# Padding the tiles that TensorE reads, so that pools begin at multiples of 128 bytes and some tiles step through the residues modulo 512

## The chip, the cores and the metric

The kernel runs on one core of a Trainium2 chip. The metric is device time in microseconds (us) of one execution. Times of single instructions are given in nanoseconds (ns). Where this text speaks of an address, it means the byte offset of a buffer within a partition of the on-chip memory (SBUF); all 128 partitions have the same layout.

## The reference, cut to what matters

One sequence of 512 tokens with 1024 channels goes through two blocks. All values are float32.

```python
# first block, layer kind 0: modulation by c, short gated convolution, squared-relu MLP
a = modulate(rmsnorm(h, g_pre), mod[0], mod[1])
h = h + mod[2] * rmsnorm(short_gated_conv(a, sc_w_in, sc_conv, sc_w_out), g_post)
f = squared_relu_mlp(modulate(rmsnorm(h, g_pre_ff), mod[3], mod[4]), mlp_w_in, mlp_w_out)
h = h + mod[5] * rmsnorm(f, g_post_ff)
# second block
x = x + even_mixer(rms_norm(x, g), ...)      # 8 heads of attention with forget gates, pooling
x = x + conv_ffn(rms_norm(x, g), ...)        # up 1024 -> 2 * 2816, 3-tap convolution, down
x = x + conformer_conv(rms_norm(x, g), ...)  # 31-tap depthwise convolution, layer norm
x = x + conv_ffn(rms_norm(x, g), ...)
```

## The kernel before, in words

**Layout.** Channels lie on the partitions and tokens along the free axis, so an activation is a list of tiles of 128 channels x 512 tokens (2048 bytes in each partition).

**Products in parts.** Every float32 product is made of three products in the type float32r. An activation is split into a high and a low part (`part_pair`, then `cut_value` or `cut_scaled`), a weight block likewise (`Stream.cut`, L86). `prod3` (L458) then issues three matmuls of 512 columns: high weight x high activation (L461), high weight x low activation (L462), low weight x high activation (L463). The weight is the stationary operand, a 128 x 128 block (512 bytes in each partition), which TensorE loads while the matmul before it runs; the activation is the moving operand, streamed in 512 columns. `in_block`, `out_block` and `late1_half` call `prod3` over the channel blocks; `lead_blocks` (L486, L487, L489), `tok_prod` (L1125 to L1127, where the weight moves and the activation stands still) and `taps` (L1632 to L1634, the depthwise convolution as products with diagonal matrices) issue the same kind of matmul by themselves.

**Names.** The tiles of the pool `xa` are the inputs of the layers: `a0h` to `a7l` in the first block, `e0h` to `e7l` before the attention, `n0h` to `n7l` before the feed-forwards and the convolution module, and `mp` for the pooled part. `h` are the hidden tiles of the first block's MLP (pool `hp`), `f` those of the two feed-forwards (pools `hp0` and `hp1`, function `ffn`, L1495), `u` those of the first output projection (pool `ua`), `s` those after the layer norm (pool `slp`). `whi` and `wlo` are the split weights (pool `wsp`, six buffers each), `ma` the attention's results, `cuh` and `cul` the inputs of the depthwise convolution with `dh` and `dl` as their diagonal weights (pool `cp`), `pth` and `ptl` the turned probabilities (pool `at`).

**Order.** The order is written out by hand. SP issues the weight loads, ScalarE and VectorE split them ahead of their use, TensorE works through the blocks. Eight PSUM banks are used in turn.

**Addresses.** Pools lie one behind the other in the order in which they are opened, from byte 1152 on; a pool that is closed gives its space to the next. Each buffer is rounded up to 32 bytes. Adding up the sizes gives where the operands of TensorE begin, modulo 512:

| operand | before, modulo 512 |
|---|---|
| `xa` tiles (`a`, `e`, `n`, `mp`), `whi`, `wlo` | 384, all of them |
| `u`, `h`, `f`, `s` | 160, all of them |
| `ma` | 448 (six), 192 (two) |
| `pth`, `ptl`, the value tiles | 480 |
| `dh`, `dl` | 96 |
| `cuh` / `cul` (a tap adds 4 bytes) | 480 and 96 / 224 and 352 |
| `identr` | 416 |

The blocks within a weight tile are 512 bytes apart, so they all have the residue of their tile.

Of the kernel before, what the change touches and what calls it, by code (L numbers as in the profile page):

```python
# [15 lines left out]
P = 128  # L16
D = 1024
T = 512
# [18 lines left out]
# columns of the packed per-channel parameters  # L37
# [14 lines left out]
# order of the first projection's blocks: c, v, b of each channel block  # L52
# [7 lines left out]
def ksplit(k0, k1):  # L60
    """pieces of at most eight k blocks"""
    n = -(-(k1 - k0) // 8)
    step = -(-(k1 - k0) // n)
    return [(k, min(k + step, k1)) for k in range(k0, k1, step)]


class Stream:
    """Weights in the order in which they are used: loaded, then split into two float32r parts."""
# [17 lines left out]
    def cut(self, n, late=False):  # L86
        """the second parts may be left for later"""
        nc = self.nc
        while self.n_cut < min(n, len(self.chunks)):
            self.load(self.n_cut + 1)  # L90
            t, w = self.staged.pop(self.n_cut)
            hi = self.pool.tile([P, 1024], F32R, tag="whi", name="whi", bufs=self.n_split)
            lo = self.pool.tile([P, 1024], F32R, tag="wlo", name="wlo", bufs=self.n_split)
            nc.scalar.copy(hi[:, :w], t[:, :w])  # L94
            self.late.append((lo[:, :w], t[:, :w], hi[:, :w].bitcast(F32)))
            self.parts[self.n_cut] = (hi, lo)
            self.n_cut += 1
        if not late:
            self.finish()
# [13 lines left out]
    def ahead(self, lag=1, late=False):  # L113
        """to be called when the products of all the chunks taken, but the last lag, have been issued"""
        self.cut(self.used + self.n_split - lag, late)
# [3 lines left out]
def fused(ctx: ExitStack, tc: tile.TileContext, a, out: bass.AP):  # L119
# [19 lines left out]
    # ---- the order in which weights are used  # L139
# [45 lines left out]
    # ---- constants and parameters  # L185
# [20 lines left out]
    par = const.tile([P, NPAR], F32, name="par")  # L206
# [25 lines left out]
    still = xa.tile([P, T], F32R, tag="xa", name="still")  # L232
# [3 lines left out]
    # ---- helpers  # L236
    def run(steps, others=()):
        """a chain of steps, with other work put between them"""
        others = list(others)
        while True:  # L240
            try:
                next(steps)
            except StopIteration as e:
                res = e.value
                break
            if others:
                others.pop(0)()
        for f in others:
            f()
        return res  # L250

    def rsqrt_steps(src, n, scale, name, late=None, eps=True, out=None):
        """1 / sqrt(src * scale + EPS): a seed from the exponent, a step of the third order, one of Newton's"""
        v = src
        if eps:
            v = small.tile([P, 64], F32, tag="rv", name="rv")[:, :n]
            V.tensor_scalar(v, src, scale, EPS, op0=ALU.mult, op1=ALU.add)
            yield
        y = small.tile([P, 64], F32, tag=f"ry{name}", name="ry")[:, :n]
        V.tensor_scalar(y.bitcast(I32), v.bitcast(I32), 1, None, op0=ALU.logical_shift_right)  # L260
        hv = small.tile([P, 64], F32, tag="rh", name="rh")[:, :n]
        V.tensor_scalar(hv, v, -9.0 / 128.0, None, op0=ALU.mult)
        yield
        V.tensor_scalar(y.bitcast(I32), y.bitcast(I32), -1.0, float(0x5F3759DF), op0=ALU.mult, op1=ALU.add)
        yield
        t = small.tile([P, 64], F32, tag="rt", name="rt")[:, :n]
        V.tensor_mul(t, y, y)
        yield
        V.tensor_mul(t, t, v)
        yield  # L270
        V.scalar_tensor_tensor(t, t, -10.0 / 3.0, t, op0=ALU.add, op1=ALU.mult)
        yield
        V.scalar_tensor_tensor(y, t, 5.0, y, op0=ALU.add, op1=ALU.mult)
        yield
        V.tensor_mul(t, y, y)
        V.tensor_scalar(y, y, 0.375, None, op0=ALU.mult)
        yield
        V.tensor_mul(t, t, hv)
        if late:
            late()  # L280
        yield
        out = y if out is None else out
        V.scalar_tensor_tensor(out, t, 1.5, y, op0=ALU.add, op1=ALU.mult)
        return out
# [4 lines left out]
    class Sums:  # L289
        """sums over the channels, by token: over the blocks first, then over the partitions"""  # L290
# [44 lines left out]
    class Total:  # L335
        """[token, tile] for a sum; the last block's terms may be added over the partitions"""
# [12 lines left out]
        def copy(self):  # L349
            self.t = small.tile([P, NT], F32, tag="tot", name="tot", bufs=6)  # L350
# [15 lines left out]
    class HalfTotals:  # L366
        """the same for several sums and a half of the tokens; t is all of them, [token, sum, tile]"""
# [41 lines left out]
    def second_norm_steps(r, sxy, syy, sxx):  # L409
        """of x + r * G y, r being y's norm: from the sums of x G y, (G y)^2 and the mean of x^2 with EPS"""  # L410
# [12 lines left out]
    def turned(r):  # L423
        """[token, tile] to [any partition, token]"""
# [13 lines left out]
    def warm(n, src):  # L438
        """n products of no use, while TensorE would wait: an idle one's clock is halved"""
# [4 lines left out]
    def part_pair(name, pool=None, tag="xa"):  # L444
        pool = pool or xa
        return (pool.tile([P, T], F32R, tag=tag, name=name + "h"), pool.tile([P, T], F32R, tag=tag, name=name + "l"))

    def cut_value(dst, src):
        """two float32r parts of src"""
# [3 lines left out]
    def cut_scaled(dst, src, g, p=P):  # L453
        """two float32r parts of src * g, g by partition"""
# [3 lines left out]
    def prod3(ps, w, o, act, first, last):  # L458
        """ps += w[:, o:o+128].T @ act, without the product of the two low parts"""
# [5 lines left out]
    def in_block(acts, between=None):  # L465
        """a block of 128 outputs over all the channel blocks"""
# [7 lines left out]
    def lead_blocks(acts_of, n):  # L474
        """n such blocks at once, channel block by channel block, as those are made"""
# [16 lines left out]
    def out_halves(acts, k0, k1):  # L492
        """the same by halves of the tokens, one after the other"""
# [18 lines left out]
    # ================= first block: modulation and the short gated convolution  # L512
    mod = const.tile([P, 48], F32, name="mod")
# [8 lines left out]
    # the modulation: a column of it on each partition, the sum over its rows along the free axis;  # L522
    # on VectorE, and up to a limit on GpSimd and ScalarE
# [11 lines left out]
    def limit(b, m):  # L535
        """of the shift all is left to GpSimd, at first a half, and of the first scale a half"""
# [31 lines left out]
    def modulated(t, sc, sh, b):  # L568
        """scaled, shifted, and the first of its two parts"""
# [6 lines left out]
    def modulated_first(t, sc, sh, b):  # L576
        """the same, the first part as early as may be"""
# [76 lines left out]
    # the rest of the modulation, in pieces between the blocks  # L654
# [66 lines left out]
    # ---- output projection, post norm, residual  # L721
# [14 lines left out]
    def sums1(b, s, ps):  # L736
        """what remains is left for VectorE"""
# [26 lines left out]
    # the last blocks, by halves of the tokens: the first half's norms are made during the second's products  # L764
# [104 lines left out]
    def second_half():  # L869
        """True before steps on TensorE"""  # L870
# [56 lines left out]
    # ================= squared relu MLP  # L927
# [45 lines left out]
    # the last blocks, by halves of the tokens: the first half's norm is made during the second's products  # L973
# [75 lines left out]
    # the first of the pooled blocks' products, by halves too  # L1049
# [10 lines left out]
    def second_half():  # L1060
        """the second half's norm, between the first half's products"""
# [55 lines left out]
    # ================= second block, layer 0: forgetting attention and pooling  # L1117
# [14 lines left out]
    # pooling  # L1132
# [18 lines left out]
    # queries and keys, raw, with the sums of squares of their heads  # L1151
    qk, ssqk = [], at.tile([P, 2 * NT * NH], F32, name="ssqk")
    rr = at.tile([P, NT], F32, name="rr")
# [16 lines left out]
    def head_norms(i):  # L1170
        """norms of the heads: of the raw sums, the token's own norm squared goes with them"""
# [38 lines left out]
    # forget gates: by head, turned to tokens  # L1210
# [26 lines left out]
    # sums of the gates over tokens  # L1237
# [14 lines left out]
    # attention, head by head  # L1252
# [23 lines left out]
    # values  # L1276
    touch = at.tile([P, 1], F32, name="touch")
# [23 lines left out]
    # values, by token  # L1301
# [11 lines left out]
    # where a tile of queries lies in three banks  # L1313
# [83 lines left out]
    # the pooled part of the output goes to the residual while heads are on their way  # L1397
# [20 lines left out]
    def residual_next(b, ps, gain):  # L1418
        """the residual with a new part, and what the next layer takes of it; its end is left for later"""
# [18 lines left out]
    # the attention's part of the output; the last two heads' products come last  # L1438
# [30 lines left out]
    # ================= gated feed-forward with a causal convolution of three taps  # L1469
    def ffn(l, next_gain):  # L1470
# [9 lines left out]
        def pair(n, pg, pv, rb):  # L1480
# [14 lines left out]
            hid[n] = part_pair(f"f{n}", hp, "hp")  # L1495
# [48 lines left out]
    # ================= layer 1: convolution module  # L1544
# [7 lines left out]
    whi = cp.tile([P, CW * KB], F32R, name="dwh", bufs=1)  # L1552
    wlo = cp.tile([P, CW * KB], F32R, name="dwl", bufs=1)
# [16 lines left out]
    # on GpSimd some taps, multiplied by ScalarE, and the bias  # L1570
# [50 lines left out]
    def taps(i, k0=0, k1=CW, between=None):  # L1621
        """some of the taps on TensorE"""
# [16 lines left out]
    def dwconv(i, k0=0, k1=CW):  # L1639
        ps, n = ps_dw[i], n_pe[i] + n_pool[i]  # L1640

        # the other taps, in two sums
# [20 lines left out]
    # the norm's sums, of the channels less their first block's mean  # L1663
# [98 lines left out]
def _blocks(w):  # L1762
    """[K, N] to [N / 128, 128 rows of a k block, K / 128 * 128]"""
# [4 lines left out]
def _columns(v):  # L1768
    """[..., n * 128] to [128, ... * n]"""
    return v.reshape(-1, P).T  # L1770
# [81 lines left out]
```

## Time and profile before

| | |
|---|---|
| median of 3 runs | 1734.66 us (1733.01 to 1735.14) |
| span of the profiled execution (first to last instruction) | 1729.1 us |
| TensorE busy with matmuls | 1699.6 us, 98% of the span, 7919 matmuls |
| VectorE, ScalarE, GpSimd busy | 1100.1, 763.3, 207.2 us |
| mean granted TensorE clock | 0.997 of full speed |

Of the profiled execution the span alone is shown; the median of the runs is 5.6 us longer than it, which is taken as what lies around the span. A matmul's duration in the profile is longer than the distance from its start to the next one's, since matmuls are pipelined and their ends are modelled: what a matmul costs is read from start to start.

### The profile page before, as it was taken

What the parts mean: (1) busy time and instruction counts of PE and PEld (TensorE: products, weight loads), DVE (VectorE), ACT (ScalarE), POOL (GpSimd) and SP (SyncE); (2) the same over time, 40 slices, a digit from 0 to 9 for tenths busy, and PEclk for the clock granted to TensorE, in tenths of its full rate; (3) what the DMA queues carried; (4) which work ended last, traced back from release to release, by engine and by line L of the source; (5) the groups of instructions that cost most, each with busy time, mean ns of one, the idle gap of its engine ahead of it and who ended that gap; (6) DMA issues with size and microseconds to landing.
All of it is one profiled execution on the core that took longest, in us unless ns stands there. A gap on an engine that the chain in (4) does not pass through costs nothing.

```text
span 1729.1 us, 20739 instructions
## 1 busy us (share of the span) xinstructions
PE 1699.6 (98%) x7919; PEld 1404.0 (81%) x7919; DVE 1100.1 (64%) x1717; ACT 763.3 (44%) x1256; POOL 207.2 (12%) x184
## 2 busy tenths in 40 slices
PE   8999899999999999999999999999999999999999
PEld 6788788888888887888888888888887888888887
DVE  6877887245244776855875377557987587636752
ACT  4533454234233335763543244347885344323430
POOL 3100630000003500000000000006880000000000
PEclk9999999999999999999999999999999999999999
DMA  7476405332323132201323322332120223232232
GB/s 290 146 262 213 139 21 177 114 104 67 123 75 96 62 105 85 74 25 49 107 93 93 122 73 90 97 119 86 50 73 1 97 86 98 91 116 95 92 97 71
DMA packets 53669, 176.13 MB, mean 102 GB/s; under 512 B 6081, under 2 KB 6337, under 8 KB 52546
## 3 DMA queue, kind: packets, MB, share of 16 engines
q1 hardware_dynamic: 53570, 174.82, 30.4%
q8 instruction: 62, 1.02, 0.2%
q14 instruction: 37, 0.30, 0.1%
HBM read 172.69 MB, written 2.10 MB: 101 GB/s over the span
## 4 chain that ended last, share of the span: by engine, by line
PE 90%; DVE 6%; ACT 1%; issue 1%; POOL 0%; DMA 0%; POOLq 0%; ACTq 0%; DVEq 0%
PE ps L461 25%; PE ps L463 25%; PE ps L462 25%; PE ps L1125 1%; PE ps L1127 1%; PE ps L1126 1%; PE ps L486 1%; PE ps L487 1%; PE ps L489 1%; PE ps_dw L1632 1%; PE ps_dw L1633 1%; PE ps_dw L1634 1%; DVE ada L533 1%; DVE wlo L103 1%; PE ps_ss L343 1%
## 5 line engine op out<-in xcount | busy, mean ns | idle before, releaser
L103 DVE TENSOR_TENSOR wlo<-stage,whi 128x1024 fp32r<-128x1024 f32 (+3 forms) x311 | 339.9, 1119 | 80.9 <-ACT whi L94 79.8
L94 ACT CAST whi<-stage 128x1024 fp32r<-128x1024 f32 (+3 forms) x313 | 288.6, 947 | 176.1 <-DMA stage<-in_down 49.8
L1486 ACT ACTIVATE zo<-z,par 128x512 f32<-128x512 f32 x88 | 70.3, 814 | 157.3 <-DVE z L1484 157.3
L1490 DVE SCALAR_TENSOR_TENSOR zo<-z,par,zo 128x510 f32<-128x510 f32 (+1 forms) x176 | 123.4, 746 | 10.8 <-ACT zo L1486 10.8
L1484 DVE TENSOR_TENSOR z<-ps,rbc 128x512 f32<-128x512 f32 x88 | 59.2, 686 | 72.4 <-PE ps L463 68.9
L306 POOL TENSOR_TENSOR acc<-acc,term 128x512 f32<-128x512 f32 (+1 forms) x34 | 45.6, 1352 | 458.1 <-ACT term L310 449.3
L1579 POOL TENSOR_TENSOR po<-po,pr 128x512 f32<-128x512 f32 x55 | 73.1, 1330 | 18.2 <-ACT pr L1578 14.5
L1493 ACT ACTIVATE zo<-zo 128x512 f32<-128x512 f32 x44 | 27.9, 633 | 66.2 <-DVE zo L1490 66.2
L533 DVE SCALAR_TENSOR_TENSOR ada<-ada,cs 128x1024 f32<-128x1024 f32 (+1 forms) x42 | 52.6, 1259 | 6.2 <-DMA ada<-in_ada 6.2
L1531 DVE TENSOR_TENSOR x<-x,ps 128x512 f32<-128x512 f32 x16 | 11.0, 688 | 71.2 <-PE ps L463 71.2
L935 DVE TENSOR_TENSOR r<-r 128x512 f32<-128x512 f32 x32 | 22.1, 690 | 47.1 <-ACT r L933 47.1
L1587 POOL MEMSET cu<- 128x30 f32 x8 | 1.0, 125 | 390.1 <-PE ps L463 390.1
L933 ACT ACTIVATE r<-ps 128x512 f32<-128x512 f32 x32 | 19.1, 595 | 61.3 <-PE ps L463 57.1
L966 DVE TENSOR_TENSOR y<-y,ps 128x512 f32<-128x512 f32 x14 | 9.6, 687 | 55.2 <-PE ps L463 55.2
L1420 DVE TENSOR_TENSOR x<-x,ps 128x512 f32<-128x512 f32 x24 | 16.4, 683 | 38.3 <-PE ps L463 38.3
L461 PE MATMUL ps<-n7h,whi 128*128 128x512 f32 x104 | 40.7, 391 | 0.0
L463 PE MATMUL ps<-n7h,wlo 128*128 128x512 f32 x104 | 40.5, 390 | 0.0
L462 PE MATMUL ps<-n7l,whi 128*128 128x512 f32 x104 | 40.5, 389 | 0.0
L1578 ACT ACTIVATE pr<-cu,par 128x512 f32<-128x512 f32 x55 | 38.9, 711 | 2.8 <-POOL po L1579 2.8
L461 PE MATMUL ps<-n0h,whi 128*128 128x512 f32 x96 | 38.2, 398 | 0.0
L463 PE MATMUL ps<-n0h,wlo 128*128 128x512 f32 x96 | 37.4, 390 | 0.0
L463 PE MATMUL ps<-n1h,wlo 128*128 128x512 f32 x96 | 37.4, 390 | 0.0
(1382 smaller groups left out, 5092.0 us busy)
## 6 DMA issues: line engine op xcount, KB each, us to landing
stage<-in_up SPq DMA_DIRECT2D x88, 512.0 KB, 3.8
ada<-in_ada SPq DMA_DIRECT2D x32, 512.0 KB, 4.6
stage<-in_mlp_in SPq DMA_DIRECT2D x32, 512.0 KB, 3.6
stage<-in_down SPq DMA_DIRECT2D x32, 384.0 KB, 3.1
stage<-in_pw SPq DMA_DIRECT2D x24, 512.0 KB, 3.7
stage<-in_down SPq DMA_DIRECT2D x32, 320.0 KB, 3.3
stage<-in_mlp_out SPq DMA_DIRECT2D x28, 320.0 KB, 3.2
stage<-in_sc_in SPq DMA_DIRECT2D x17, 512.0 KB, 3.7
```

Source lines behind the costliest of these rows:

```text
L94: nc.scalar.copy(hi[:, :w], t[:, :w])
L103: (engine or self.nc.vector).tensor_sub(lo, t, hi)
L306: self.engine.tensor_add(self.acc[:, s], self.acc[:, s], t)
L461: PE.matmul(ps, hi, act[0], start=first, stop=False)
L462: PE.matmul(ps, hi, act[1], start=False, stop=False)
L463: PE.matmul(ps, lo, act[0], start=False, stop=last)
L533: V.scalar_tensor_tensor(t[:, s], t[:, s], 1.0, cs[:, s], op0=ALU.mult, op1=ALU.mult, accum_out=to)
L1484: V.tensor_mul(z, ps, rb)
L1486: S.activation(o, z, AF.Identity, bias=col(fcb, j), scale=col(fcw, 2 * 2 * FB + j))
L1490: V.scalar_tensor_tensor(o[:, s:], z[:, :T - s], col(fcw, (2 - s) * 2 * FB + j), o[:, s:], op0=ALU.mult, op1=ALU.add)
L1578: S.activation(pr, u, AF.Copy, scale=w)
L1579: G.tensor_add(po[i], po[i], pr)
```

## The change

Nothing is computed otherwise, and no instruction is added, removed or moved. Tiles become longer:

- `par`, `mod`, `rr`, `touch` (of the pool `at`), `dwh`, `dwl` and the tag `tot` (nine buffers for six) are lengthened, so that the pools behind them begin at multiples of 128 bytes.
- `whi` and `wlo` get 64 bytes more each, tiles of `xa` 32 bytes more, the `f` tiles (now under the tag `fp`) 32 bytes more; the `f` tiles with an odd number begin 16 bytes into their buffer.

```diff
+LINE = 32
...
-            hi = self.pool.tile([P, 1024], F32R, tag="whi", name="whi", bufs=self.n_split)
-            lo = self.pool.tile([P, 1024], F32R, tag="wlo", name="wlo", bufs=self.n_split)
+            hi = self.pool.tile([P, 1024 + 16], F32R, tag="whi", name="whi", bufs=self.n_split)
+            lo = self.pool.tile([P, 1024 + 16], F32R, tag="wlo", name="wlo", bufs=self.n_split)
...
-    par = const.tile([P, NPAR], F32, name="par")
+    par = const.tile([P, -(-NPAR // LINE) * LINE], F32, name="par")[:, :NPAR]
...
-    still = xa.tile([P, T], F32R, tag="xa", name="still")
+    still = xa.tile([P, T + 8], F32R, tag="xa", name="still")[:, :T]
...
-            self.t = small.tile([P, NT], F32, tag="tot", name="tot", bufs=6)
+            self.t = small.tile([P, NT], F32, tag="tot", name="tot", bufs=9)
...
-        pool = pool or xa
+        if pool is None or tag == "fp":
+            wide = (pool or xa).tile
+            o = 4 * (int(name[1:]) % 2) if tag == "fp" else 0
+            return tuple(wide([P, T + 8], F32R, tag=tag, name=name + p)[:, o:o + T] for p in "hl")
         return (pool.tile([P, T], F32R, tag=tag, name=name + "h"), pool.tile([P, T], F32R, tag=tag, name=name + "l"))
...
-    mod = const.tile([P, 48], F32, name="mod")
+    mod = const.tile([P, 56], F32, name="mod")[:, :48]
...
-    rr = at.tile([P, NT], F32, name="rr")
+    rr = at.tile([P, LINE], F32, name="rr")[:, :NT]
...
-    touch = at.tile([P, 1], F32, name="touch")
+    touch = at.tile([P, LINE], F32, name="touch")[:, :1]
...
-            hid[n] = part_pair(f"f{n}", hp, "hp")
+            hid[n] = part_pair(f"f{n}", hp, "fp")
...
-    whi = cp.tile([P, CW * KB], F32R, name="dwh", bufs=1)
-    wlo = cp.tile([P, CW * KB], F32R, name="dwl", bufs=1)
+    whi = cp.tile([P, 8 * LINE], F32R, name="dwh", bufs=1)[:, :CW * KB]
+    wlo = cp.tile([P, 8 * LINE], F32R, name="dwl", bufs=1)[:, :CW * KB]
```

The removed comments and docstrings are left out here. Adding up the new sizes in the same way gives:

| operand | after, modulo 512 |
|---|---|
| `xa` tiles, the sixteen buffers | 0, 32, 64, ... 480, one each |
| `whi`, the six buffers | 0, 64, 128, 192, 256, 320 |
| `wlo`, the six buffers | 384, 448, 0, 64, 128, 192 |
| `u`, `h`, `s` | 128, all of them |
| `f`, the 24 buffers | 128, 160, 192, ... in steps of 32; 16 more for an odd number |
| `ma` | 0 (six), 256 (two) |
| `pth`, `ptl`, the value tiles | 128 |
| `dh`, `dl` | 128 |
| `cuh` / `cul` (a tap adds 4 bytes) | 0 and 128 / 256 and 384 |
| `identr` | 0 |

## Rows read from the trace of the kernel before

**Rows 1.** The page, part 1: busy us, share of the span, instructions.
```profile
PE 1699.6 (98%) x7919; PEld 1404.0 (81%) x7919; DVE 1100.1 (64%) x1717; ACT 763.3 (44%) x1256; POOL 207.2 (12%) x184
```

**Rows 2.** The page, part 4: shares of the chain that ended last.
```profile
PE 90%; DVE 6%; ACT 1%; issue 1%; POOL 0%; DMA 0%; POOLq 0%; ACTq 0%; DVEq 0%
```

**Rows 3.** Groups by line, PE: shapes, count, then busy us and mean ns.
```profile
L461 PE MATMUL ps<-n7h,whi 128*128 128x512 f32 x104 | 40.7, 391 | 0.0
L463 PE MATMUL ps<-n7h,wlo 128*128 128x512 f32 x104 | 40.5, 390 | 0.0
...
L462 PE MATMUL ps<-n3l,whi 128*128 128x512 f32 x96 | 37.3, 389 | 0.0
...
L461 PE MATMUL ps<-a1h,whi 128*128 128x512 f32 x44 | 17.1, 390 | 0.0
...
L1127 PE MATMUL ps<-whi,e5l 128*128 128x512 f32 x12 | 4.7, 390 | 0.0
```

**Rows 4.** The same view, the `f` tiles: first and last kind.
```profile
L461 PE MATMUL ps<-f1h,whi 128*128 128x512 f32 x16 | 6.3, 395 | 0.0
...
L463 PE MATMUL ps<-f21h,wlo 128*128 128x512 f32 x15 | 5.9, 395 | 0.0
```

**Rows 5.** One tile's instructions, `h5h`, `s1h`: count, duration min/median/max ns.
```profile
L461 PE MATMUL ps<-h5h,whi x8: 393/395/397, 296.5 to 350.4; 128*128 128x512 f32 x8
...
L461 PE MATMUL ps<-s1h,whi x4: 396/396/396, 1339.9 to 1356.7; 128*128 128x512 f32 x4
```

**Rows 6.** Timeline of PE (start us, us), from 999.76 us on.
```profile
999.76 0.39 PE L461 MATMUL ps<-n5h,whi 128*128 128x512 f32 x1
999.99 0.39 PE L462 MATMUL ps<-n5l,whi 128*128 128x512 f32 x1
...
1008.83 0.39 PE L462 MATMUL ps<-n2l,whi 128*128 128x512 f32 x1
```

**Rows 7.** Timeline of PE, from 923.84 us on.
```profile
923.84 0.40 PE L461 MATMUL ps<-f0h,whi 128*128 128x512 f32 x1
...
932.48 0.40 PE L462 MATMUL ps<-f1l,whi 128*128 128x512 f32 x1
```

**Rows 8.** Timeline of PE in the attention's output, from 781.55 us on.
```profile
781.55 0.39 PE L461 MATMUL ps<-ma,whi 128*128 128x512 f32 x1
...
788.88 0.39 PE L463 MATMUL ps<-ma,wlo 128*128 128x512 f32 x1
```

**Rows 9.** Timeline of PE in the depthwise taps, from 1231.82 us on.
```profile
1231.82 0.39 PE L1632 MATMUL ps_dw<-cuh,dh 128*128 128x512 f32 x1
...
1235.77 0.40 PE L1634 MATMUL ps_dw<-cuh,dl 128*128 128x512 f32 x1
```

**Rows 10.** Two tiles' instructions: the least and the greatest durations.
```profile
L462 PE MATMUL ps<-n0l,whi x96: 387/389/398, 815.2 to 1658.9; 128*128 128x512 f32 x96
...
L1633 PE MATMUL ps_dw<-cul,dh x83: 389/396/404, 1179.3 to 1306.8; 128*128 128x512 f32 x83
```

**Rows 11.** Timeline of PE, matmuls of 256 columns, `u` and `a` tiles.
```profile
192.97 0.28 PE L461 MATMUL ps<-u0h,whi 128*128 128x256 f32 x1
...
193.91 0.28 PE L463 MATMUL ps<-u2h,wlo 128*128 128x256 f32 x1
...
240.14 0.28 PE L915 MATMUL ps<-a7h,whi 128*128 128x256 f32 x1
...
240.98 0.28 PE L915 MATMUL ps<-a0h,whi 128*128 128x256 f32 x1
```

**Rows 12.** Stretches: length, then busy us (instructions) of PE, granted clock, DMA.
```profile
924.00:980.00 56.00, 56.00 (x242) 1.00 0.33 102
1000.00:1080.00 80.00, 80.00 (x354) 1.00 0.27 88
```

## Prediction

> **What bounds the kernel now.** I read the busy times first. TensorE is busy with matmuls for 98% of the span, and the next engine, VectorE, for 64% [rows 1]. The chain that ended last says the same from its end: 90% of it is TensorE, and no line of it is a transfer [rows 2]. So TensorE's stream of matmuls is the kernel, and a change that adds, removes and moves no instruction can act on the time in one way alone: by the distance from the start of one matmul to the start of the next. The granted clock is 1.00 in the stretches that I compare, so this is the 2.4 GHz level throughout [rows 12]; 512 columns at 2.4 GHz are 213.3 ns, one column in a cycle.
>
> The next view is the grouping by line with shapes kept apart. The same three lines issue the same 128 x 512 matmul all over the kernel, and yet two levels show: 389 to 391 ns where the moving tile is `n`, `a` or a weight against `e` [rows 3], 395 ns where it is `f` [rows 4], and 395 to 396 ns where it is `h` or `s` [rows 5]. The ends are modelled, so I take the starts from the timeline. From 999.76 to 1008.83 us there are 40 steps of `n` matmuls: 9.07 / 40 = 226.75 ns [rows 6]. From 923.84 to 932.48 us there are 37 steps of `f`: 8.64 / 37 = 233.5 ns [rows 7]. A duration in these rows is thus some 162 ns more than the step, in both groups. The attention's output has 32 steps of `ma` in 7.33 us, 229.1 ns [rows 8], and the depthwise taps 17 steps in 3.95 us, 232.4 ns [rows 9].
>
> What differs between these groups is not the weight's address, which is 384 modulo 512 for `n`, `f` and `ma` alike, but the moving tile's: 384 for `n` and `a` (a multiple of 128, and the weight's own residue), 448 and 192 for `ma` (odd multiples of 64), 160 for `f`, `h`, `s` and `u` (an odd multiple of 32), and anything in steps of 4 bytes for the taps. By rows, then: multiples of 128 cost 226.75 ns, odd multiples of 64 cost 229.1, odd multiples of 32 cost 233.5, a mixture 232.4.
>
> **The change part by part.** The pads of `par`, `mod`, `tot`, `rr`, `touch`, `dwh` and `dwl` cost nothing themselves: no instruction reads the added bytes, and VectorE, ScalarE and the transfers handle as many elements as before. The three more buffers of `tot` could only remove waits, and on the chain that ended last TensorE waits for almost nothing. What they do is to move what lies behind them. Four groups of matmuls come out of this.
>
> *Group 1, what reads `xa`.* Counting the rows of the grouped view, 2519 matmuls of 512 columns read `n`, 1224 `a`, 96 `mp` and 48 `e` as moving operand, and 288 have `e` as the standing one: 4175. Today both operands are at 384. Afterwards the sixteen buffers step by 32, so that half of the tiles stand at multiples of 64 and half at odd multiples of 32, and the weights at multiples of 64. For the first half I take the middle of the two rows, (226.75 + 229.1) / 2 = 227.9 ns, for the second half 233.5 ns [rows 6 to 8]; the mean is 230.7 ns. That is 3.95 ns more in each of 4175: +16.5 us.
>
> *Group 2, `h`, `s` and `u`.* 708 + 192 + 120 = 1020 matmuls of 512 columns move from 160 to 128, with weights at multiples of 64: from 233.5 to 227.9 ns, -5.6 ns each, -5.7 us.
>
> *Group 3, `f`.* 1023 matmuls. Of an even-numbered pair one tile is at a multiple of 64 and the other at an odd multiple of 32, 230.7 ns as in group 1; the odd-numbered pairs begin 16 bytes off, and the nearest row is that of the taps, 232.4 ns [rows 9]. The mean, 231.5 ns, is 2.0 ns less than today: -2.0 us.
>
> *Group 4, the rest.* In the taps, weights and moving tiles shift by the same 32 bytes, so they keep their distance; I leave them at nothing, and 249 of them at 1 ns would be 0.25 us. Some 710 matmuls have 256 columns: those of `u` now take 0.94 us for 8 steps, 117.5 ns, those of `a` 0.84 us for 7, 120 ns [rows 11]. These levels stand the other way round than at 512 columns; a change of 2.5 ns in all of them would be 1.8 us either way, and I take nothing.
>
> The sum is 16.5 - 5.7 - 2.0 = +8.8 us. The profiled execution's span of 1729.1 us becomes 1737.9, and with the 5.6 us that the median has beyond that span, 1743.5 us.
>
> The bounds. No row shows varied addresses in the order that the change makes, where the distance between weight and moving tile is another one in nearly every matmul. The dearest nearby view is that nothing settles and all matmuls of groups 1 to 3 cost what `f` costs now: 6.75 x 4175 = +28.2 us, 1763 us. With the taps' 232.4 ns in group 1 and the rest as above it is +23.6 - 7.7 = +15.9 us, 1750.6 us. The cheapest is the least duration on record, 387 ns against a usual 389 [rows 10], a step of some 224.7 ns: with that everywhere, 2.05 x 4175 + 8.8 x 2043 = 8.6 + 18.0 = 26.6 us less, 1708 us. I take the middle values because they are the rows of steady stretches; the greatest durations of the taps, 404 ns [rows 10], are single ones.
>
> **The rivals.** *The equal residues are the trouble, and spreading them is the cure (faster).* A step of 226.75 ns is 13.4 ns more than the columns need, although nothing is waited for. If that excess arises where the weight's read meets the moving tile's read at the same residue, then `xa` pays it in every matmul today and will pay less afterwards. For it speaks that at 256 columns the unequal pair (160 and 384) takes 117.5 ns and the equal one 120 [rows 11]. Against it: at 512 columns every unequal pair on record is dearer than the equal one [rows 6 to 9]. It decides the sign when group 1 comes to less than 226.75 + 7.7 / 4.175 = 228.6 ns; with the least step on record throughout, it gives 1708 us. The Trainium skill (page "TensorE: Matmul & The Clock Gate", section "Wait — 56ns, not 53.3ns?") gives about 215.7 ns for back-to-back matmuls of 512 columns at the full clock; no step of 512 columns in this trace is as short, and by that figure the sum would be near 1652 us, an estimate.
>
> *Only the alignment counts, and the spread is harmless (faster, smaller).* Then `xa` stays at 226.75 ns, group 2 gains up to 6.75 ns, 6.9 us, and group 3 between 2.0 and 6.9 us: 1721 to 1726 us, 1723 in the middle. It wants a tile at an odd multiple of 32 to cost no more than one at 384, which `f`, `h` and `s` deny with their weights at 384; with the weights of other residues it is not shown.
>
> *Addresses have no effect (the same).* The two levels would then come from what else runs beside the matmuls. Against it, `n` and `f` alternate within the same feed-forward, at a similar share of the transfers, 0.27 and 0.33 [rows 12], and `h` and `s`, in other stages with other neighbours, have the level of `f` [rows 5]. It gives 1734.7 us. The Trainium skill (same page, section "Step-by-step: what each phase is for") says that TensorE reads its standing and its moving operand through two independent ports, so that loading the next weights takes no read bandwidth from the running matmul. By that rule no residue could matter and the sum would be zero; the trace does not agree, with 226.75 against 233.5 ns for the same instruction.
>
> **How the numbers follow.** The slower case has 0.48: the rows carry it, but its largest term rests on pairs of addresses that no row shows. The first rival has 0.19, the second 0.23, the third 0.10. So faster by over 0.2% (3.5 us, about what a measurement of this kernel tells from no change) is 0.42, within it 0.10, slower 0.48. The predicted time is that of the likeliest case, 1743.5 us; its own range is 1738 to 1757 us. The range that should hold 8 in 10 has to take in both signs: from 1708, the cheapest case, to 1757 us, short of the dearest bound.
>
> **What would show it.** If I am right, the rows of `n` and `a` in the grouped view rise from 389 to some 393 ns and differ from tile to tile, those of `h`, `s` and `u` fall to 390 to 391, those of `f` to 393, and the steps in the timeline follow. VectorE's, ScalarE's and the transfers' times do not change. I am wrong if the `n` rows stay at 389 (second rival) or fall below it (first), or if `h` stays at 395, which would mean that the multiple of 128 was not what made `n` cheap.

## The result, and the profile after

The changed kernel takes 1747.76 us (median of 4 runs, 1745.41 to 1749.85) against 1733.84 us of the kernel before (4 runs, 1730.77 to 1735.14): a ratio of 1.0091, 95% interval 1.0079 to 1.0103, slower by 0.9%. The prediction was 1743.5 us and slower. The medians differ by 13.9 us, and the interval stands for 13.7 to 17.9 us. The span of the profiled execution grew by 16.9 us, from 1729.1 to 1746.0 us; the mean granted clock of these two executions was 0.997 and 0.992.

The page of the changed kernel, parts 1 and 4, which answer to [rows 1, 2]:

```profile
PE 1715.8 (98%) x7919; PEld 1406.6 (81%) x7919; DVE 1102.0 (63%) x1717; ACT 763.0 (44%) x1256; POOL 208.7 (12%) x184
...
PE 91%; DVE 6%; ACT 1%; issue 1%; POOL 0%; DMA 0%; POOLq 0%; ACTq 0%; DVEq 0%
```

The same number of instructions on every engine, and TensorE alone is longer: by 16.2 us, nearly all of the span's 16.9. The weight loads are not (1404.0 before, 1406.6 now). So the place to look is the step from one matmul to the next, as before. The groups by line, which answer to [rows 3, 4]; the edit moves the lines by five, so that `prod3` is now at L466 to L468:

```profile
L466 PE MATMUL ps<-n7h,whi 128*128 128x512 f32 x104 | 41.0, 394 | 0.0
...
L467 PE MATMUL ps<-n3l,whi 128*128 128x512 f32 x96 | 37.8, 394 | 0.0
...
L466 PE MATMUL ps<-a1h,whi 128*128 128x512 f32 x44 | 17.4, 396 | 0.0
...
L468 PE MATMUL ps<-f21h,wlo 128*128 128x512 f32 x15 | 5.9, 396 | 0.0
...
L1132 PE MATMUL ps<-whi,e5l 128*128 128x512 f32 x12 | 4.7, 395 | 0.0
```

The 389 to 391 ns of `n`, `a` and `e` have become 394 to 396; `f` stands where it stood. Two tiles' instructions (least, median and greatest duration), which answer to [rows 5]:

```profile
L466 PE MATMUL ps<-h5h,whi x8: 392/394/398, 296.3 to 349.8; 128*128 128x512 f32 x8
...
L466 PE MATMUL ps<-s1h,whi x4: 392/398/404, 1352.3 to 1369.1; 128*128 128x512 f32 x4
```

`h` and `s`, now at a multiple of 128, have not come down to 390: the medians were 395 and 396 and are 394 and 398, only with more spread. The timeline gives the steps. For `n` (compare [rows 6]) two rounds of 24 matmuls, for `f` [rows 7] 61 steps, for `h` five rounds of 33:

```profile
1007.97 0.39 PE L466 MATMUL ps<-n0h,whi 128*128 128x512 f32 x1
...
1019.08 0.40 PE L466 MATMUL ps<-n0h,whi 128*128 128x512 f32 x1
```

```profile
930.81 0.40 PE L466 MATMUL ps<-f1h,whi 128*128 128x512 f32 x1
...
944.93 0.40 PE L467 MATMUL ps<-f10l,whi 128*128 128x512 f32 x1
```

```profile
296.27 0.39 PE L466 MATMUL ps<-h5h,whi 128*128 128x512 f32 x1
...
334.53 0.40 PE L466 MATMUL ps<-h5h,whi 128*128 128x512 f32 x1
```

`n`: 11.11 / 48 = 231.5 ns, where it was 226.75. `f`: 14.12 / 61 = 231.5 ns, where it was 233.5. `h`: 38.26 / 165 = 231.9 ns; the same five rounds took 38.50 us before, 233.3 ns. The granted clock is 1.00 in these stretches, the 2.4 GHz level, so the columns still take 213.3 ns. Three groups with three different layouts have ended at one level, some 231.5 to 232 ns. With the counts of the prediction that is 4.75 x 4175 = +19.8 us for group 1, -1.4 x 1020 = -1.4 us for group 2 and -2.0 x 1023 = -2.0 us for group 3: +16.4 us, and the span has grown by 16.9. The stretches are typical: over all steps under 300 ns in the two traces `n` goes from 226.9 to 231.8 ns in the mean, `a` from 227.0 to 232.0, `h` from 233.4 to 231.5 and `f` from 233.4 to 231.8.

### The profile page after: what moved, and what is told of

Read it like the earlier page. It is cut to its first block, busy times and chain, and to the rows that moved or that the text cites. A ratio compares the mean times of both kernels' runs of the same rounds, so it can differ in the third digit from the quotient of the medians.

```text
span 1746.0 us, 20739 instructions
## 1 busy us (share of the span) xinstructions
PE 1715.8 (98%) x7919; PEld 1406.6 (81%) x7919; DVE 1102.0 (63%) x1717; ACT 763.0 (44%) x1256; POOL 208.7 (12%) x184
## 4 chain that ended last, share of the span: by engine, by line
PE 91%; DVE 6%; ACT 1%; issue 1%; POOL 0%; DMA 0%; POOLq 0%; ACTq 0%; DVEq 0%
PE ps L466 25%; PE ps L467 25%; PE ps L468 25%; PE ps L1130 1%; PE ps L1131 1%; PE ps L1132 1%; PE ps L491 1%; PE ps L492 1%; PE ps L494 1%; PE ps_dw L1637 1%; PE ps_dw L1638 1%; PE ps_dw L1639 1%; DVE ada L538 1%; DVE wlo L105 1%; PE ps_w L444 1%
## 5 line engine op out<-in xcount | busy, mean ns | idle before, releaser
L466 PE MATMUL ps<-n7h,whi 128*128 128x512 f32 x104 | 41.0, 394 | 0.0
L468 PE MATMUL ps<-n7h,wlo 128*128 128x512 f32 x104 | 41.0, 394 | 0.0
L1425 DVE TENSOR_TENSOR x<-x,ps 128x512 f32<-128x512 f32 x24 | 16.5, 686 | 37.6 <-PE ps L468 37.5
L466 PE MATMUL ps<-n0h,whi 128*128 128x512 f32 x96 | 38.4, 400 | 0.0
L467 PE MATMUL ps<-n5l,whi 128*128 128x512 f32 x96 | 38.0, 395 | 0.0
L467 PE MATMUL ps<-n6l,whi 128*128 128x512 f32 x96 | 37.9, 395 | 0.0
```

The source lines that it names most:

```text
L466: PE.matmul(ps, hi, act[0], start=first, stop=False)
L467: PE.matmul(ps, hi, act[1], start=False, stop=False)
L468: PE.matmul(ps, lo, act[0], start=False, stop=last)
```

## The theories and the experiments

**Level.** The prediction's own view: each matmul costs what the alignment of its moving tile's own address makes it cost (multiple of 128 cheap, odd multiple of 32 dear). The unmoved level of `h` speaks against it.

**Distance.** In the kernel before, all weights that meet `n`, `f` and `ma` stand at 384. A moving tile at 384, 160 or 192 is thus also one at a distance of 0, of an odd multiple of 32, or of an odd multiple of 64 from its weight. The rows of before cannot tell the two apart. By the distance theory it is this difference that counts, not any boundary.

### Operands alone: `residues`

No computation of the reference is left in this kernel: sixteen moving tiles and sixteen weights, one for each multiple of 32 modulo 512, and nothing but matmuls of 512 columns. Its core:

```python
for s in (0, 32):                       # a kept pair: 32 matmuls each
    for r in range(0, 512, 32):
        ps = bank()
        for _ in range(32):
            PE.matmul(ps, w[s], m[r], start=True, stop=True)                       # L58
...
PE.matmul(ps, w[0], m[i * 32 % 512], start=True, stop=True)    # L62, 48 times; by 64, 128, 256: L65, L68, L71
...
PE.matmul(ps, w[i * 32 % 512], m[0], start=True, stop=True)    # L75; by 64: L78
...
PE.matmul(ps, w[i * 32 % 512], m[i * 32 % 512], start=True, stop=True)         # L88; by 64, 128: L91, L94
...
PE.matmul(ps, w[(i - 1) * 32 % 512], m[i * 32 % 512], start=True, stop=True)   # L101
```

> This kernel leaves the whole computation out and runs matmuls of 512 columns on tiles at known addresses modulo 512: first one pair of weight and moving tile, kept for 32 matmuls (weight at 0 or 32, moving tile at 0, 32, ... 480), then sequences of 48 in which the moving tile, the weight, or both step by 32, 64, 128 or 256 bytes. Theory 'level' (a matmul costs by the moving tile's own alignment): kept pairs with the weight at 0 take 226.75 ns from start to start for a moving tile at a multiple of 128 bytes (duration 389), 229 ns at odd multiples of 64 (391), 233.5 ns at odd multiples of 32 (395 to 396); a stepping sequence takes the mean of the levels that it visits, so 226.75 ns for steps of 128 and 256, and a stepping weight costs nothing. Theory 'distance' (a kept distance from weight to moving tile settles into a cheap cycle, a distance that changes from matmul to matmul does not settle): kept pairs differ by distance, and every stepping sequence takes 231 to 233 ns whatever the step, 128 and 256 too, unless both step alike, which stays at 227 ns.

The timeline of this kernel cut to four stretches inside the kept pairs. The first row is moving tile 0 with weight 0, the second 32 with 0, the third 0 with 32, the fourth 32 with 32:

```profile
14.79 6.96 PE L58 MATMUL ps<-m,w 128*128 128x512 f32 x30
...
22.05 7.16 PE L58 MATMUL ps<-m,w 128*128 128x512 f32 x30
...
133.66 7.16 PE L58 MATMUL ps<-m,w 128*128 128x512 f32 x30
...
141.12 6.98 PE L58 MATMUL ps<-m,w 128*128 128x512 f32 x30
```

Each row is 29 steps and one last duration of 0.39 us: (6.96 - 0.39) / 29 = 226.6 ns, then 233.4, 233.4 and 227.2. A tile at an odd multiple of 32 is dear beside a weight at 0 and cheap beside a weight at 32; a tile at 0 is dear beside a weight at 32. For a pair that is kept, the boundary does not count, the distance does.

The timeline of the same kernel as a whole (granted clock 1.00 in these rows), one row for each line (start, length, count):

```profile
14.56 237.92 PE L58 MATMUL ps<-m,w 128*128 128x512 f32 x1024
252.31 11.40 PE L62 MATMUL ps<-m,w 128*128 128x512 f32 x48
263.55 11.29 PE L65 MATMUL ps<-m,w 128*128 128x512 f32 x48
274.68 11.20 PE L68 MATMUL ps<-m,w 128*128 128x512 f32 x48
285.72 11.08 PE L71 MATMUL ps<-m,w 128*128 128x512 f32 x48
296.64 11.39 PE L75 MATMUL ps<-m,w 128*128 128x512 f32 x48
307.87 11.28 PE L78 MATMUL ps<-m,w 128*128 128x512 f32 x48
318.98 11.31 PE L81 MATMUL ps<-m,w 128*128 128x512 f32 x48
...
341.03 11.40 PE L88 MATMUL ps<-m,w 128*128 128x512 f32 x48
352.27 11.13 PE L91 MATMUL ps<-m,w 128*128 128x512 f32 x48
363.24 11.12 PE L94 MATMUL ps<-m,w 128*128 128x512 f32 x48
374.20 11.06 PE L97 MATMUL ps<-m,w 128*128 128x512 f32 x48
385.11 11.25 PE L101 MATMUL ps<-m,w 128*128 128x512 f32 x48
396.19 11.29 PE L104 MATMUL ps<-m,w 128*128 128x512 f32 x48
```

From one row's start to the next, over 48: a moving tile that walks by 32 (L62) costs 234.2 ns a step, by 64 231.9, by 128 230.0, by 256 227.5. A weight that walks by 32 (L75) costs 234.0, by 64 231.5. Moving by 256 changes next to nothing. And the first row, all sixteen tiles with both weights, comes to 237.75 / 1024 = 232.2 ns: the mean over all distances is near the level at which the three groups of the changed kernel stand.

The distance theory missed here too. It expected 227 ns where both operands step alike, since every matmul then has distance 0 to its own weight. By 32 (L88) the step is 234.2 ns, as dear as when one operand walks alone; by 64 (L91) it is 228.5, by 128 (L94) 228.3. Where each tile has instead the residue of the next matmul's weight (L101, by 32), it is 230.8. So distance 0 is cheap when the residue also stays; a distance taken within each matmul alone does not give the step.

### Parts of the change alone: `xa_only`, `w_only`, `pads_only`

`xa_only`, the tiles of `xa` 32 bytes longer and nothing else:

```diff
-    still = xa.tile([P, T], F32R, tag="xa", name="still")
+    still = xa.tile([P, T + 8], F32R, tag="xa", name="still")[:, :T]
...
-        pool = pool or xa
+        if pool is None:
+            return tuple(xa.tile([P, T + 8], F32R, tag=tag, name=name + p)[:, :T] for p in "hl")
```

> The kernel before with the xa tiles alone lengthened by 32 bytes: they step through all sixteen residues, weights stay at 384, h, f, s and u at 160. Level: half of the xa tiles cost 227.9 ns and half 233.5 ns, by their buffer: 4175 matmuls at +3.95 ns, +16.5 us, ratio 1.0095; the rows of one a tile show 389 or 395 ns, by its buffer. Distance: all of them at some 232 ns, +5.2 ns, +21.7 us, ratio 1.0125, and the rows of all a tiles at 393 to 395 ns. Both: h, f, s, u unchanged at 395 ns.

1752.76 us against 1731.86 of the kernel before, run again beside these three, 1.0118 (1.0101 to 1.0136): the level theory's number lies outside the interval, the distance theory's inside. The two numbers lie close together, so the next two kernels have to decide.

`w_only`, the weights 64 bytes longer and nothing else; every `xa` tile keeps its 384:

```diff
-            hi = self.pool.tile([P, 1024], F32R, tag="whi", name="whi", bufs=self.n_split)
-            lo = self.pool.tile([P, 1024], F32R, tag="wlo", name="wlo", bufs=self.n_split)
+            hi = self.pool.tile([P, 1024 + 16], F32R, tag="whi", name="whi", bufs=self.n_split)
+            lo = self.pool.tile([P, 1024 + 16], F32R, tag="wlo", name="wlo", bufs=self.n_split)
```

> The kernel before with the split weights alone lengthened by 64 bytes: whi and wlo stand at multiples of 64, xa tiles all stay at 384; what lies behind the weights moves by 256 bytes, so h, f, s and u stand at 416, again an odd multiple of 32. Level: xa matmuls stay at 226.75 ns or rise to 227.9 at most, h, f, s, u stay at 233.5: 0 to +5 us, ratio 1.000 to 1.003. Distance: within each three products the weight goes from one residue to another and back, so xa matmuls cost 230 to 232 ns, +13 to +22 us, ratio 1.008 to 1.013, with no tile of the xa pool touched.

1750.84 us, 1.0107 (1.0089 to 1.0124). No moving tile of `xa` has moved, all are at a multiple of 128, and the kernel is slower by about as much as when they all move.

`pads_only`, the change without its lengthened `xa`, weight and `f` tiles: the operands listed in the tables above begin at multiples of 128, `xa` and weights at 0, `h`, `f`, `s`, `u` at 384.

```diff
-    par = const.tile([P, NPAR], F32, name="par")
+    par = const.tile([P, 864], F32, name="par")[:, :NPAR]
...
-            self.t = small.tile([P, NT], F32, tag="tot", name="tot", bufs=6)
+            self.t = small.tile([P, NT], F32, tag="tot", name="tot", bufs=9)
...
-    mod = const.tile([P, 48], F32, name="mod")
+    mod = const.tile([P, 56], F32, name="mod")[:, :48]
```

`rr`, `touch`, `dwh` and `dwl` are lengthened as in the change.

> The pads of the change alone, with nothing lengthened: xa tiles and weights all at 0, h, f, s and u at 384, every one a multiple of 128, distances kept in all stages. Level: h, f, s, u fall from 233.5 to 226.75 ns, 2043 matmuls at -6.75 ns, -13.8 us, ratio 0.992. Distance: xa stays at 226.75; h, f, s, u have a kept distance of 384, whose cost no row of before shows: between 226.75 and 233.5 ns, -13.8 to 0 us, ratio 0.992 to 1.000.

1731.61 us, 0.9997 (0.9988 to 1.0006). The level theory wanted 0.992 and falls here: 2043 matmuls went from an odd multiple of 32 to a multiple of 128 and gained nothing, since their distance went from 32 to 128 modulo 256. A kept distance of 128 costs 232.5 ns in the kernel `fine` below (its L95 starts at 156.45 us, the next line at 165.75), hardly less than 32.

One tile's instructions in the three kernels, `xa_only` first, then `w_only`, then `pads_only` with a second tile:

```profile
L463 PE MATMUL ps<-n0l,whi x96: 388/397/397, 826.5 to 1682.4; 128*128 128x512 f32 x96
```

```profile
L462 PE MATMUL ps<-n0l,whi x96: 387/393/398, 824.1 to 1680.6; 128*128 128x512 f32 x96
```

```profile
L462 PE MATMUL ps<-n0l,whi x96: 389/389/398, 814.4 to 1657.9; 128*128 128x512 f32 x96
...
L461 PE MATMUL ps<-h5h,whi x8: 392/395/398, 296.0 to 349.9; 128*128 128x512 f32 x8
```

`n0l` had a median of 389 ns [rows 10]. It rises when it moves, and as well when only its weight moves; in `pads_only`, where both moved together, it keeps 389, and `h5h` keeps its 395 at an aligned address.

### The distance made 0 everywhere: `matched`

The theory names a cure that the change does not contain: leave `xa` and the weights alone, and shift the later pools so that `h`, `f`, `s` and `u` get the residue of their weights.

```diff
     small = ctx.enter_context(tc.tile_pool(name="small", bufs=2))
+    small.tile([P, 56], F32, tag="gap", name="gap", bufs=1)
...
-    rr = at.tile([P, NT], F32, name="rr")
+    rr = at.tile([P, 60], F32, name="rr")[:, :NT]
```

> The kernel before with two tiles made longer and nothing else: 224 bytes ahead of the pools that hold h, f, s and u, which move from 160 to 384 modulo 512, the residue of their weights, and rr longer, so that ma lands at 128 and 384. The distance theory (what counts is the distance from the weight's address to the moving tile's, modulo 256, at best 0): h, f, s and u, 2043 matmuls of 512 columns, fall from 233.4 to 226.7 ns, 13.7 us less in all, and ma by 2 ns in 32 or so; a ratio of 0.992, some 1720 us. The level theory in its first form (a multiple of 128 is what makes a step cheap) would give the same here, but has to explain why h, f, s and u at the same residue 384 gained nothing where xa and the weights stood at 0. A third view, that h, f, s and u are dear for what runs beside them in their stages, expects no change, 1.000.

1719.84 us (5 runs) against 1730.86 of the kernel before, run again beside it, a ratio of 0.9931 (0.9917 to 0.9945): faster than both kernels, by one pad of 224 bytes and a longer `rr`. Groups by line, tiles, and two starts of `f`, two rounds of 33 matmuls apart:

```profile
L462 PE MATMUL ps<-f1h,whi 128*128 128x512 f32 x16 | 6.2, 389 | 0.0
```

```profile
L462 PE MATMUL ps<-h5h,whi x8: 389/389/389, 293.1 to 345.5; 128*128 128x512 f32 x8
...
L462 PE MATMUL ps<-s1h,whi x4: 389/389/389, 1331.7 to 1348.0; 128*128 128x512 f32 x4
```

```profile
919.77 0.39 PE L462 MATMUL ps<-f0h,whi 128*128 128x512 f32 x1
...
934.73 0.39 PE L462 MATMUL ps<-f0h,whi 128*128 128x512 f32 x1
```

14.96 / 66 = 226.7 ns for `f`, and every one of the eight `h5h` and four `s1h` takes 389: the level of `n`, in other stages with other neighbours. That also rules out the third view in the expectation. At 2043 x 6.7 ns the steps give back 13.7 us; the span fell by 12.1 and the medians differ by 11.0. Some of the gap is seen in a window (length, busy times, then the granted clock, DMA share and GB/s):

```profile
560.00:610.00 50.00, 45.88 (x323) 43.74 (x322) 39.08 (x97) 17.05 (x32) 21.34 (x25) 0.90 0.14 44
```

The same stretch of the kernel before has 0.97: this execution spent more time at 1.2 GHz around the start of the second block, where TensorE is busy for 45.88 of 50 us. Whether that belongs to the shifted addresses or to this one execution was not tried. A little more may be the 330 matmuls of 256 columns of `u`, `h` and `f`, for which distance 0 is the dearer one by 1.5 ns (`fine`, below): 0.5 us, an estimate.

### Which period: `whi_256`

```diff
-            hi = self.pool.tile([P, 1024], F32R, tag="whi", name="whi", bufs=self.n_split)
+            hi = self.pool.tile([P, 1024 + 64], F32R, tag="whi", name="whi", bufs=self.n_split)
```

> The kernel before with the whi buffers 256 bytes longer: they now lie at 128 and 384 modulo 512 by turns, and nothing behind them moves modulo 512. With 64 bytes more in each weight buffer the time rose by 1.1%. The distance theory with a period of 256 bytes expects no change, 1.000 (0.998 to 1.002): all distances stay 0 modulo 256. A theory in which any variation modulo 512 costs something expects 232 instead of 226.7 ns in the two thirds of 4175 matmuls that use or load whi, 10 to 20 us more, a ratio of 1.006 to 1.012.

1731.30 us (10 runs) against 1730.86, 1.0001 (0.9992 to 1.0011): addresses that vary modulo 512 cost nothing here, where every residue is kept modulo 256. The row of `n0l` is that of before [rows 10]:

```profile
L462 PE MATMUL ps<-n0l,whi x96: 387/389/398, 815.0 to 1658.6; 128*128 128x512 f32 x96
```

### Finer distances, smaller operands: `fine`

```python
for _ in range(40):
    PE.matmul(ps[:128, :512], w[:, :128], m[:, 1:513], start=True, stop=True)   # L53: 4 bytes off
```

The same for each distance, weight width and number of columns, a line for each.

> Leaves the whole computation out: 40 matmuls at a time with one weight tile at 0 modulo 512 and a moving tile at a kept distance of 0 to 256 bytes, in steps down to 4 bytes; then with 64 and 32 weight columns at distances 0, 32, 64 and 128, and with 384, 256 and 128 moving columns at the same distances. If what costs time is the reading of the next weight in the middle of the moving tile's reading, a weight of 64 or 32 columns is read in a half or a quarter of the time, and the excess over 213.3 ns (13.4 at distance 0, 20 at 32) falls by a half and three quarters. If the excess belongs to the moving tile's reading alone, it stays at 13 and 20 ns. By the 32-byte steps, no distance is below 226.6 ns; distances off the multiples of 32 are expected between 226.6 and 234.3. A theory in which only multiples of 32 bytes are clean expects all of 4, 8, 16, 24 and 28 at one level above 233.

Its timeline, one row for each line, at a granted clock of 1.00; the step is the distance to the start of the next line's row, over 40. L50 is a distance of 0, L53 of 4 bytes, L65 of 28, L68 of 32, L77 of 60, L80 of 64, L116 of 256; L120 and L132 have 64 and 32 weight columns at distance 0:

```profile
17.38 9.23 PE L50 MATMUL ps<-m,w 128*128 128x512 f32 x40
26.44 9.62 PE L53 MATMUL ps<-m,w 128*128 128x512 f32 x40
35.91 9.49 PE L56 MATMUL ps<-m,w 128*128 128x512 f32 x40
...
63.83 9.24 PE L65 MATMUL ps<-m,w 128*128 128x512 f32 x40
72.90 9.49 PE L68 MATMUL ps<-m,w 128*128 128x512 f32 x40
82.23 9.55 PE L71 MATMUL ps<-m,w 128*128 128x512 f32 x40
...
100.94 9.24 PE L77 MATMUL ps<-m,w 128*128 128x512 f32 x40
110.02 9.31 PE L80 MATMUL ps<-m,w 128*128 128x512 f32 x40
119.17 9.62 PE L83 MATMUL ps<-m,w 128*128 128x512 f32 x40
...
221.53 9.24 PE L116 MATMUL ps<-m,w 128*128 128x512 f32 x40
230.60 9.36 PE L120 MATMUL ps<-m,w 128*64 128x512 f32 x40
239.80 9.39 PE L123 MATMUL ps<-m,w 128*64 128x512 f32 x40
...
267.33 9.42 PE L132 MATMUL ps<-m,w 128*32 128x512 f32 x40
276.60 9.48 PE L135 MATMUL ps<-m,w 128*32 128x512 f32 x40
```

Distance 0: 9.06 / 40 = 226.5 ns, the 512 columns' 213.3 and 13.2 more; 4 bytes: 236.8; 28: 226.8; 32: 233.3; 60: 227.0; 64: 228.8; 256: 226.8. So multiples of 32 are not special either: 28 and 60 are as cheap as 0, and 4 bytes off is the dearest in this list. At 512 columns nothing is cheaper than distance 0. With 64 weight columns a step at distance 0 takes 9.20 / 40 = 230.0 ns, with 32 columns 231.8. At distance 0 a shorter weight read thus does not shrink the excess, it raises it. At distance 32 the step falls a little, from 233.3 to 230.8 ns with 64 columns (L123, 239.80 to 249.03 us) and to 232.8 with 32, so neither form of the expectation holds. With fewer moving columns the order changes: at 384 the steps at distance 0 and 32 are alike, 173.5 and 173.3 ns (L145, L148), and at 256 distance 0 is the dearest, 119.5 against 118.0 ns at 32 and 117.8 at 64 (L157, L160, L163). The theory that all distances off the multiples of 32 are alike and dear falls too. What TensorE's two reads do to each other within a step stays open.

## Why the prediction was right in sign, and where it was not

*What bounds the kernel:* right. No instruction was added, and TensorE's busy time carries 16.2 of the 16.9 us.

*Group 1, what reads `xa`:* right in sign and kind, too small in size. The step rose from 226.75 to 231.5 ns, 4.75 against the 3.95 forecast, 19.8 us against 16.5. This term was mis-sized. The forecast gave half of the tiles 227.9 ns for standing at multiples of 64. There is no such half: any one tile meets weights at all multiples of 64, so that its distance changes with the weight, and what the group pays is near the mean over distances, 232.2 ns in the operand kernel. The prediction had named this gap (pairs of addresses that no row shows), and its own alternative with the taps' 232.4 ns was the nearer row. One reading was off from the start: `mp`, counted at 226.75 ns, took 229.7 ns a step in the mean already in the kernel before (see the last section).

*Group 2, `h`, `s`, `u`:* this step failed. "From 233.5 to 227.9 ns" rests on the multiple of 128 being what made `n` cheap; the rows after show 231.9, and `pads_only` shows that alignment to 128 by itself gives 0.9997. `n` was cheap because it stood, matmul after matmul, at the residue of its weights. The prediction had set down this sign: `h` staying at 395.

*Group 3, `f`:* -2.0 us forecast, -2.0 by the stretch of 61 steps (-1.6 over all 1023), but by another route than the split into even and odd pairs: `f` too came near the mean over distances. That the number fits is luck.

*Group 4:* nothing was seen that the sums need; 0.5 of the span's 16.9 us is not assigned. As the two executions also differ in granted clock, an agreement this close is partly chance.

*The sum:* 8.8 us forecast against 16.9 in the span. The 8.1 us between are 3.3 of group 1 and 4.3 of group 2, and that remainder. The two errors have one root, the level read as a property of one operand.

*From span to median:* the 5.6 us taken as what lies around the span are wrong. In the changed kernel the profiled execution took 1747.74 us with a span of 1746.0, 1.7 us more, and every run on record with its span is 1.7 or 1.8 us longer than it. The other 3.9 us are the distance of the profiled execution (1730.77 us) from the median of three others. So the forecast of 1743.5 us came within 4.3 us of the measured median by luck: the term hid about half of the 8.1 us that the sum was short.

*The rivals.* Equal residues as the trouble: at 512 columns the reverse holds, equal and kept is the cheapest, and `matched` gains by making them equal. Its one row for it was real: with 256 columns the unequal pair is the cheaper one [rows 11], and `fine` shows the same without the kernel around it. Only the alignment counts: refuted by `pads_only` and `w_only`. No effect of addresses: refuted by `residues`, `xa_only`, `w_only` and `matched`. The Trainium skill (page "TensorE: Matmul & The Clock Gate", section "Step-by-step: what each phase is for") has the two operands read through independent ports, so that loading the next weights takes no read bandwidth from the running matmul. Read as a rule that no address matters, the runs do not agree: `w_only` lengthens the weights alone, and the kernel takes 1.07% longer. Whether it is the reading that is slowed, no run shows.

## What to carry to other kernels

Where weight loads alternate with full 512-column float32r matmuls in long runs, give the weights and the moving tiles one common residue modulo 256, and lengthen tiles only by multiples of 256. A boundary alone gave nothing, walking through the residues made every group pay about the mean, and equal residues within each pair did not help where they changed from pair to pair by 32. At 256 columns the equal residue was the dearer one, so measure there. When a trace holds only a few pairs of addresses, write down both readings, absolute and relative, before pricing one of them: here the rows of before on which the terms rest fitted both. A level that depends on placement is cheaply tested by a kernel that holds nothing but the operands.

## What the runs showed of the hardware

- The step of a 512-column float32r matmul with its weight load is 226.6 ns in long runs at a kept distance of 0 modulo 256, some 229 at 64 and 233.3 at 32. With weight and tile both at 32 it is 227.2. With the weight at 0, 28 and 60 bytes are as cheap as 0, and 4 bytes cost 236.8.
- A short run need not reach that level. In the kernel before, `mp` stands at the residue of its weights and comes twelve matmuls at a time between the attention's own; its steps after the first lie between 224 and 236 ns in the first such run, the last three at 226 and 227, and one of its tiles shows a median of 395 ns where `n` has 389:

```profile
L461 PE MATMUL ps<-mp1h,whi x8: 387/395/397, 700.2 to 762.4; 128*128 128x512 f32 x8
```

- One operand that walks by 32, 64 or 128 from matmul to matmul costs 230.0 to 234.2 ns a step; by 256 it is 227.5. Both walking alike cost 228.3 to 234.2.
- At 256 columns distance 0 is the dearest of those tried: 119.5 ns against 117.8 to 118.5 at 32, 64 and 128.
- The 13.3 ns above the columns' own 213.3 are there even at the best distance, and a weight of 32 columns does not lessen them (231.8 ns). The Trainium skill (same page, section "Wait — 56ns, not 53.3ns?") has 215.7 ns for back-to-back matmuls of 512 columns; the nearest step measured here at a kept pair is 226.5 ns, and for this kernel the measured one decides.
- Open: by what mechanism addresses act. Neither the distance to the weight in use (0 in L88 of `residues`, 234.2 ns) nor that to the next matmul's weight (0 in L101, 230.8 ns) gives the step by itself.
